# A uniform offset of 192 bytes for all split weights in SBUF

## The chip, the core and the metric

One core of one Trainium2 chip runs the whole program in one launch. The metric is the device time of that core in microseconds, from repeated runs of the same program; the profile is taken in one more execution of it.

## What is computed

The input is x of 256 tokens by 1024 features, float32. There are two layers. Each has a token mixer and a gated feed-forward net (FFN), each behind an RMS norm and added back to x; a last norm ends it.

```python
for i in range(2):
    h = rmsnorm(x, mix_norm[i])
    x = x + (short_conv_mixer(h) if i == 0 else moba_attention(h))
    x = x + conv_ffn(rmsnorm(x, ffn_norm[i]), w_up[i], w_conv[i], w_down[i])
return rmsnorm(x, final_norm)
# short_conv_mixer: b, c, v = split(h @ w_in); (b * causal_conv3(c * v)) @ w_out
# conv_ffn: g, u = split(causal_conv3(h @ w_up)); (silu(g) * u) @ w_down      (2816 wide)
# moba_attention: 16 heads of 64, rotary positions; with 256 tokens there is
#   one block, so it is plain causal softmax attention
```

## The kernel before

Activations lie with features on the 128 partitions and 256 tokens along the free dimension. Float32 accuracy is reached with three float32r products: weight and activation are each split into a high part (rounded to float32r) and a low part (the rest), and `passes` (line 304) issues high x high, high x low and low x high into the same PSUM bank.

The weights come as units of 128 x 1024 floats (the first eleven are smaller), two units to a load (`load_chunk`, line 154; four chunks are in flight). `split_next` (line 174) splits one unit: ScalarE writes `hi`, VectorE writes `lo`. The splits live in `SPLITS` = 5 buffers each. A matmul takes 128 columns of a unit, 512 bytes per partition, as its stationary operand (its weights) and streams 256 columns of an activation. Two products do it the other way round, with 512 columns of a weight unit moving past 128 columns of an activation: v of the attention (`v_stage`, line 645) and the down-projection of layer 1 (`TokenAccum`, line 351).

The stages follow each other in program order, and each engine works in that order (`InOrder`, line 87): the load phase with the first rounds of the mixer (`firsts`), then its rounds j = 2 to 7 (tiles cv and b, 48 and 24 products a round; mo is its output projection, 24 a round), the norm's sum of squares (`finish_norm`, tile ss: products with a 128 x 128 tile of ones, `ones_r`, as weights), the FFN of layer 0 (gu is the up-projection, 48 products for each of 22 j; fo is the down-projection, 24 for each j, which starts when j = 4 is through), the attention (q and k in tile qk, v, then scores s, transposes pt and value products o in plain float32, by four groups of heads; ao is its output projection), and the FFN of layer 1. The count of float32r products with 256 columns is 3992: 576 of cv and b, 192 of mo, 1056 of gu and 528 of fo in layer 0, 384 of qk, 192 of ao, 1056 of gu in layer 1, and 8 of ss. With 512 columns there are 360: 96 of v and 264 of fo in layer 1.

Where an operand begins in SBUF is set by `line` (line 135): it makes a tile that is `off` floats longer and rounds it up to `LINE` = 128 floats, and hands out the part behind `off`. The pools begin at a multiple of 512 bytes, so a tile's place relative to such a multiple is its `off`. For weights that is `WEIGHTS_AT` (line 37), by the kind of unit; for activations it is 0 everywhere. `ones_r` happens to begin 384 bytes behind a multiple. In bytes:

| products | stationary operand begins at | moving operand begins at |
|---|---|---|
| cv, b (and the load phase) | 64 | 0 |
| mo | 128 | 0 |
| gu, layer 0 | 192 | 0 |
| fo, layer 0 | 256 | 0 |
| q / k | 320 / 384 | 0 |
| v | 0 | 256 |
| ao | 448 | 0 |
| gu, layer 1 | 480 | 0 |
| fo, layer 1 | 0 | 128 |
| ss | 384 | 0 |

Since 128 columns are 512 bytes, every slice of a unit has the offset of the unit. All instructions carry line 97 in the profile (the helper `InOrder` issues them), so they are told apart by the names of their tiles.

Of the kernel before, what the change touches and what calls it, by code (L numbers as in the profile page):

```python
# [9 lines left out]
F32 = mybir.dt.float32  # L10
F32R = mybir.dt.float32r
# [3 lines left out]
P = 128  # L15
D = 1024
T = 256
# [7 lines left out]
U = 1024  # L25
# [2 lines left out]
NG = 4  # L28
GROUPS = 4
LOADS = 4  # L30
SPLITS = 5
NBIG = 14
NT = 10
LINE = 128


WEIGHTS_AT = {"first": 16, "in": 16, "out": 32, "up0": 48, "down0": 64, "q": 80, "k": 96, "v": 64, "o": 112, "up1": 120, "down1": 32}
INPUTS_AT = {0: 0, "out": 0, 1: 0, "down0": 0, 2: 0, "o": 0, 3: 0, "down1": 0}
NPS = 7
WARM = 8  # L40

# [32 lines left out]
PLAN = weight_plan()  # L74
# [39 lines left out]
def trunk(ctx: ExitStack, tc: tile.TileContext, x, wall, small, ropes, masks, final, out):  # L114
# [15 lines left out]
    rope = cp.tile([P, 3, T], F32, name="rope")  # L130
    mk = cp.tile([P, P + T], F32, name="mk")
    ones = cp.tile([P, P], F32, name="ones")
    ones_r = cp.tile([P, P], F32R, name="ones_r")

    def line(pool, w, off=0, dtype=F32, **kw):

        return pool.tile([P, -(-(off + w) // LINE) * LINE], dtype, **kw)[:, off : off + w]

    def gain(i, m):
        return gn_c[:, i * ND + m : i * ND + m + 1]  # L140
# [11 lines left out]
    raw, hi, lo = {}, {}, {}  # L152
# [21 lines left out]
    def split_next():  # L174
        u = state["split"]
        if u >= NU:
            return
        state["split"] += 1
        c, o = CHUNK_OF[u]
        while state["dma"] <= min(c + LOADS - 1, len(CHUNKS) - 1):  # L180
            load_chunk()
        w = WIDTH[u]
        src = raw[c][:, o : o + w]
        kind = PLAN[u][0] + (str(PLAN[u][1]) if PLAN[u][0] in ("up", "down") else "")
        hi[u], lo[u] = (
            line(wp, U + 127 - WEIGHTS_AT[kind], WEIGHTS_AT[kind], F32R, name=f"{n}{u}", tag=n, bufs=SPLITS)[:, :w]
            for n in ("hi", "lo")
        )
        if u < 2:
            V.tensor_copy(hi[u], src)  # L190
            if u == 0:
                scaled(0, (0,), nm0)
                split_next()
                for v, part in ((0, src), (1, raw[0][:, P : 3 * P])):
                    V.tensor_sub(lo[v], part, hi[v].bitcast(F32))
            return
        S.activation(hi[u], src, AF.Copy)
        V.tensor_sub(lo[u], src, hi[u].bitcast(F32))
# [10 lines left out]
    def spawn(*gens):  # L209
        tasks.extend(gens)  # L210
# [43 lines left out]
    def scaled(i, ms, nm):  # L254

        for m in ms:
            xh, xl = (
                line(ap_, T, INPUTS_AT[i], F32R, name=f"x{c}{i}_{m}", tag=f"x{c}{m}", bufs=1)
                for c in "hl"
            )  # L260
            S.activation(xh, xslice(m), AF.Copy, scale=gain(i, m))
            V.scalar_tensor_tensor(
                xl, xslice(m), gain(i, m), xh.bitcast(F32), op0=ALU.mult, op1=ALU.subtract
            )
            nm.xh[m], nm.xl[m] = xh, xl
# [12 lines left out]

    def table(func):

        t = line(ap_, 1, name="table", tag="table", bufs=1)
        S.activation(t, ones[:, 0:1], func)

    def finish_norm(i, nm, squared=False, cols=False, tag="b"):

        ps = bank(f"ss{i}", tag=tag)
        for part, total in enumerate(nm.total):
            kw = {"start": False, "stop": part == 1, "skip_group_check": True}
            E.matmul(ps[:, 0, :], ones_r, total, **{**kw, "start": part == 0})
            for t in range(2 if cols else 0):  # L290
                E.matmul(
                    ps[:, 1, 2 * t : 2 * t + 2], total[:, t * P : (t + 1) * P], ones_r[:, 0:2], **kw
                )
        n = T + 4 if cols else T
        rms = line(ap_, T + 4, name=f"rms{i}", tag="rms", bufs=1)
        ss = ps.rearrange("p a t -> p (a t)")[:, :n]
        S.activation(rms[:, :n], ss, AF.Sqrt, bias=eps, scale=1.0 / D)
        nm.r = line(ap_, T + 4, name=f"rstd{i}", tag="rstd", bufs=2)
        V.reciprocal(nm.r[:, :n], rms[:, :n])
        if squared:  # L300
            nm.r2 = ap_.tile([P, T], F32, name=f"rstd2{i}", tag="rstd2", bufs=1)
            V.tensor_mul(nm.r2, nm.r[:, :T], nm.r[:, :T])
# [131 lines left out]
    def pair_tile(name):  # L434
        return ap_.tile([P, 2, T], F32, name=name, tag="big", bufs=NBIG)

    def split_tiles(name, kind):
        return tuple(
            line(ap_, T, INPUTS_AT[kind], F32R, name=name + c, tag="ps" + c, bufs=NPS) for c in "hl"
        )  # L440

    def taps(y, src, w):
# [4 lines left out]


    V.memset(ones, 1.0)
    eps = cp.tile([P, 32], F32, name="eps")[:, 0:1]  # L450
    V.memset(eps, EPS)
    V.tensor_copy(ones_r, ones)
    o = NG * ND
# [31 lines left out]
    def mix_b(j, b_ps, in_y, wait=1):  # L485
        for _ in range(wait):
            yield
        yb = half_tile(f"yb{j}")
        V.tensor_mul(yb, b_ps[:, 0, :], in_y[0])
        yield  # L490
        ys[j] = split_tiles(f"ys{j}", "out")
        split_act(*ys[j], yb)

    firsts = [(bank(f"cv{j}", tag="a"), bank(f"b{j}", tag="a")) for j in range(2)]
# [55 lines left out]
    def ffn(layer, nm, i, then):  # L550
        acc, ps = (TokenAccum if then is None else Accum)(f"fo{layer}"), {}
        gus = {}

        def whole(j):
            gn, y = pair_tile(f"gn{layer}_{j}"), pair_tile(f"gy{layer}_{j}")
            s, p = half_tile(f"s{layer}_{j}"), half_tile(f"p{layer}_{j}")
            V.tensor_mul(gn, gus[j], nm.r[:, None, :T].to_broadcast([P, 2, T]))
            yield
            for h in range(2):
                taps(y[:, h, :], gn[:, h, :], lambda t: ffn_tap(layer, t, h, j))  # L560
            yield
            S.activation(s, y[:, 0, :], AF.Silu)
            V.tensor_mul(p, s, y[:, 1, :])
            yield
            ps[j] = split_tiles(f"ps{layer}_{j}", f"down{layer}")
            split_act(*ps[j], p)

        for j in range(NF):
            if layer == 0 and j == 2:
                Q.dma_start(rope, ropes)  # L570
                Q.dma_start(mk, masks)
            gu = gus[j] = bank(f"gu{layer}_{j}")
            wg, wu = unit(("up", layer, 0, j)), unit(("up", layer, 1, j))
            if j == 0:
                for ks in ((0, 1), (2, 3), (4, 5), (6, 7)):
                    project(gu[:, 0, :], wg, nm, ks)
                    project(gu[:, 1, :], wu, nm, ks, start=False)
                slot()
                slot()
            else:  # L580
                project(gu[:, 0, :], wg, nm)
                slot()
                project(gu[:, 1, :], wu, nm, start=False)
                if j == 1:
                    finish_norm(i, nm)
                    table(AF.Silu)
                    spawn(whole(0))
                spawn(whole(j))
                slot()
            if j >= LAG_FFN:  # L590
                acc.add(("down", layer, j - LAG_FFN), ps[j - LAG_FFN], j == LAG_FFN, False)
                slot()
        for j in range(NF - LAG_FFN, NF - 2):
            acc.add(("down", layer, j), ps[j], False, False)
            slot()
        while tasks:
            slot(0)
        table(AF.Sqrt)
        acc.finish(
            [("down", layer, j) for j in (NF - 2, NF - 1)],  # L600
            [ps[j] for j in (NF - 2, NF - 1)],
            then,
        )
# [89 lines left out]
    def softmax(g, ps):  # L693
        sm = [pair_tile(f"sm{g}_{h}").rearrange("p a t -> p (a t)") for h in range(4)]
        mx, nmx, sums, inv = (
            line(ap_, 8, name=f"{n}{g}", tag=n) for n in ("mx", "nmx", "sums", "inv")
        )
        parts = [(2 * h + t, h, slice(c0, c1)) for h in range(4) for c0, c1, t in SPANS]
        for c, h, cols in parts:
# [33 lines left out]
    def values(g, now=False):  # L733
        pt = pts.pop(g)
        o = bank(f"o{g}")
        for e in range(2):
            for t in range(2):
                for h in (2 * e, 2 * e + 1):
                    E.matmul(
                        o[h % 2 * HD : (h % 2 + 1) * HD, e, t * P : T],  # L740
                        vt[t][:, 4 * g + h, :],
                        pt[h][:, T * t : T * t + (T if t == 0 else P)],
                        start=e == 0 and t == 0,
                        stop=t == 1,
                        skip_group_check=True,
                    )
        hl = [
            line(ap_, 2 * T, INPUTS_AT["o"], F32R, name=f"o{c}{g}", tag=f"o{c}{g}", bufs=1)
            .rearrange("p (a t) -> p a t", a=2)
            for c in "hl"  # L750
        ]
        for e in range(2):
            os_[2 * g + e] = tuple(v[:, e, :] for v in hl)

        def split_values():
            split_act(*hl, o)
            yield

        spawn(split_values())
        if now:  # L760
            next(tasks[-1])
# [145 lines left out]
```

## Time and profile before

| | us |
|---|---|
| median of 3 runs | 583.34 (582.89 to 583.95) |
| the profiled execution | 582.72 |
| its span, first to last instruction | 580.9 |
| mean granted clock of TensorE | 0.998 of full speed |

Three views matter here. The page's head gives each engine's busy time. The waits of an engine say what held it up. The chain that ended last, in order of time, merges like instructions that follow each other on it, and says of each run when it starts, how long it takes and how many there are: a run's length divided by its count is the time from one matmul's start to the next. (The duration that the profile gives for one matmul, some 278 ns, overlaps with its neighbours.)

### The profile page before, as it was taken

What the parts mean: (1) busy time and instruction counts of PE and PEld (TensorE: products, weight loads), DVE (VectorE), ACT (ScalarE), POOL (GpSimd) and SP (SyncE); (2) the same over time, 40 slices, a digit from 0 to 9 for tenths busy, and PEclk for the clock granted to TensorE, in tenths of its full rate; (3) what the DMA queues carried; (4) which work ended last, traced back from release to release, by engine and by line L of the source; (5) the groups of instructions that cost most, each with busy time, mean ns of one, the idle gap of its engine ahead of it and who ended that gap; (6) DMA issues with size and microseconds to landing.
All of it is one profiled execution on the core that took longest, in us unless ns stands there. A gap on an engine that the chain in (4) does not pass through costs nothing.

```text
span 580.9 us, 11291 instructions
## 1 busy us (share of the span) xinstructions
PE 573.9 (99%) x4628; PEld 552.9 (95%) x4628; DVE 470.4 (81%) x783; ACT 338.0 (58%) x556; POOL 8.7 (2%) x12
## 2 busy tenths in 40 slices
PE   9999999999999999999999999999999999999996
PEld 8999999999999999999989997999999999999984
DVE  6997768899978877886998887577998878877883
ACT  7654447567655555555846656565665555555543
POOL 0022010000000000000000000000000000000000
PEclk9999999999999999999999999999999999999999
DMA  8957561746645546455264344463566455564301
GB/s 305 371 206 247 189 217 73 259 155 243 247 162 212 185 178 217 155 210 192 103 230 156 119 146 146 146 228 116 186 225 220 161 209 177 186 210 159 140 1 72
DMA packets 17188, 106.86 MB, mean 184 GB/s; under 512 B 1904, under 2 KB 3056, under 8 KB 4976
## 3 DMA queue, kind: packets, MB, share of 16 engines
q1 hardware_dynamic: 16704, 105.60, 51.1%
q8 instruction: 36, 0.59, 0.4%
q10 hardware_dynamic: 432, 0.54, 0.3%
q14 instruction: 16, 0.13, 0.1%
HBM read 105.09 MB, written 1.05 MB: 183 GB/s over the span
## 4 chain that ended last, share of the span: by engine, by line
PE 97%; DMA 1%; SPq 0%; ACT 0%; DVE 0%; issue 0%; ACTq 0%
PE gu L97 42%; PE fo L97 22%; PE qk L97 8%; PE cv L97 7%; PE ao L97 4%; PE mo L97 4%; PE v L97 4%; PE b L97 4%; PE pt L97 1%; PE s L97 1%; PE o L97 1%; DMA raw<-wall 1%; SPq L97 0%; PE ss L97 0%; ACT hi L97 0%; ACT of L97 0%
## 5 line engine op out<-in xcount | busy, mean ns | idle before, releaser
L97 ACT ACTIVATE hi<-raw 128x1024 fp32r<-128x1024 f32 (+2 forms) x199 | 205.5, 1041 | 155.3 <-PE gu L97 83.6
L97 DVE TENSOR_TENSOR lo<-raw,hi 128x1024 fp32r<-128x1024 f32 (+3 forms) x201 | 239.9, 1200 | 61.1 <-ACT hi L97 60.8
L97 PE MATMUL gu<-xl,hi 128*128 128x256 f32 x704 | 195.8, 278 | 0.0
L97 PE MATMUL gu<-xh,hi 128*128 128x256 f32 x704 | 195.7, 278 | 0.0
L97 PE MATMUL gu<-xh,lo 128*128 128x256 f32 x704 | 195.7, 278 | 0.0
L97 PEld LDWEIGHTS gu<-xh,hi 128*128 128x128 f32 x704 | 132.3, 188 | 0.7
L97 PEld LDWEIGHTS gu<-xl,hi 128*128 128x128 f32 x704 | 132.2, 188 | 0.7
L97 PEld LDWEIGHTS gu<-xh,lo 128*128 128x128 f32 x704 | 132.2, 188 | 0.0
L97 DVE SCALAR_TENSOR_TENSOR gy<-gn,sm,gy 128x255 f32<-128x255 f32 (+1 forms) x176 | 80.8, 481 | 3.1
L97 ACT ACTIVATE gy<-gn,sm 128x256 f32<-128x256 f32 x88 | 39.3, 497 | 6.4 <-DVE gn L97 6.4
L97 PE MATMUL qk<-xh,hi 128*128 128x256 f32 x128 | 36.4, 284 | 0.0
L97 PE MATMUL qk<-xl,hi 128*128 128x256 f32 x128 | 35.8, 280 | 0.0
L97 PE MATMUL qk<-xh,lo 128*128 128x256 f32 x128 | 35.8, 280 | 0.0
L97 DVE TENSOR_TENSOR gn<-gu,rstd 128x512 f32<-128x512 f32 x44 | 30.1, 689 | 6.5 <-PE gu L97 6.5
L97 PE MATMUL cv<-xh,hi 128*128 128x256 f32 x128 | 33.3, 281 | 0.4 <-ACT hi L97 0.4
L97 PE MATMUL cv<-xl,hi 128*128 128x256 f32 x128 | 32.9, 278 | 0.0
L97 PE MATMUL cv<-xh,lo 128*128 128x256 f32 x128 | 32.8, 277 | 0.0
L97 PEld LDWEIGHTS qk<-xh,hi 128*128 128x128 f32 x128 | 24.2, 189 | 0.5 <-issue 0.3
L97 PEld LDWEIGHTS qk<-xl,hi 128*128 128x128 f32 x128 | 24.1, 188 | 0.0
L97 PEld LDWEIGHTS qk<-xh,lo 128*128 128x128 f32 x128 | 24.1, 188 | 0.0
L97 PEld LDWEIGHTS cv<-xh,hi 128*128 128x128 f32 x128 | 23.1, 189 | 0.7 <-ACT hi L97 0.6
L97 ACT ACTIVATE s<-gy 128x256 f32<-128x256 f32 x44 | 17.9, 406 | 9.4 <-DVE gy L97 9.2
(474 smaller groups left out, 1081.7 us busy)
## 6 DMA issues: line engine op xcount, KB each, us to landing
raw<-wall SPq DMA_DIRECT2D x95, 1024.0 KB, 4.7
raw<-wall SPq DMA_DIRECT2D x6, 384.0 KB, 6.7
xt<-x SPq DMA_DIRECT2D x3, 256.0 KB, 6.1
out<-of SPq DMA_DIRECT2D x3, 256.0 KB, 2.1
raw<-wall SPq DMA_DIRECT2D x3, 192.0 KB, 4.2
gain_row<-final SPq DMA_DIRECT2D x1, 512.0 KB, 5.7
rope<-ropes SPq DMA_DIRECT2D x1, 384.0 KB, 5.9
out<-of ACTq DMA_DIRECT2D x1, 256.0 KB, 2.4
```

The costliest lines, as they stand in the source:

```text
L97: r = f(*args, **kw)
```

## The change

All split weights get one offset. The table `WEIGHTS_AT`, the table `INPUTS_AT` and the helper `line` go. Instead the tiles of constants that come first are sized so that what follows falls into place: `eps` is made 80 floats (320 bytes) long and is allocated ahead of `ones_r`, so that `ones_r`, and with it everything behind it in the pools of constants and weights, begins 192 bytes beyond a multiple of 512; the tile `table`, the first of the activations' pool, is 80 floats long too, and 192 + 320 = 512 brings all activations back to a multiple. The raw (unsplit) weights, `vt` and `gain_row` also lie at 192 now. Without the padding a split buffer is 4096 bytes instead of 4608, and there are six of each kind instead of five. The order of instructions on each engine and their number are as before; the inner function `whole` of the FFN is renamed `gated`, since `whole` now names the helper that rounds a tile up to 128 floats.

```diff
-SPLITS = 5
+SPLITS = 6
-LINE = 128
-WEIGHTS_AT = {"first": 16, "in": 16, "out": 32, "up0": 48, "down0": 64, "q": 80, "k": 96, "v": 64, "o": 112, "up1": 120, "down1": 32}
-INPUTS_AT = {0: 0, "out": 0, 1: 0, "down0": 0, 2: 0, "o": 0, 3: 0, "down1": 0}
...
     ones = cp.tile([P, P], F32, name="ones")
+    eps = cp.tile([P, 80], F32, name="eps")[:, 0:1]
     ones_r = cp.tile([P, P], F32R, name="ones_r")
-    def line(pool, w, off=0, dtype=F32, **kw):
-        return pool.tile([P, -(-(off + w) // LINE) * LINE], dtype, **kw)[:, off : off + w]
+    def whole(pool, w, **kw):
+        return pool.tile([P, -(-w // 128) * 128], F32, **kw)[:, :w]
...
-        kind = PLAN[u][0] + (str(PLAN[u][1]) if PLAN[u][0] in ("up", "down") else "")
-        hi[u], lo[u] = (
-            line(wp, U + 127 - WEIGHTS_AT[kind], WEIGHTS_AT[kind], F32R, name=f"{n}{u}", tag=n, bufs=SPLITS)[:, :w]
-            for n in ("hi", "lo")
-        )
+        hi[u] = wp.tile([P, w], F32R, name=f"hi{u}", tag="hi", bufs=SPLITS)
+        lo[u] = wp.tile([P, w], F32R, name=f"lo{u}", tag="lo", bufs=SPLITS)
...
-        t = line(ap_, 1, name="table", tag="table", bufs=1)
+        t = ap_.tile([P, 80], F32, name="table", tag="table", bufs=1)[:, 0:1]
...
-    eps = cp.tile([P, 32], F32, name="eps")[:, 0:1]
```

## Rows read from the trace of the kernel before

**Rows 1.** The page's head: busy us, share of the span, count.

```profile
span 580.9 us, 11291 instructions
...
PE 573.9 (99%) x4628; PEld 552.9 (95%) x4628; DVE 470.4 (81%) x783; ACT 338.0 (58%) x556; POOL 8.7 (2%) x12
```

**Rows 2.** The waits of TensorE: us in total, times, longest us.

```profile
PE busy L97 <- DVE eps L97: 1.1, 1, 1.1
PE cv L97 <- ACT hi L97: 0.4, 1, 0.4
```

**Rows 3.** The chain in order of time: start us, length us, what, count.

```profile
3.53 5.06 DMA raw<-wall
...
22.36 5.65 PE cv L97 x48
...
53.18 5.46 PE cv L97 x48
...
83.40 11.39 PE mo L97 x96
94.78 11.31 PE gu L97 x96
...
126.16 5.44 PE gu L97 x48
...
264.72 14.40 PE fo L97 x120
279.12 8.51 PE qk L97 x72
291.17 10.90 PE v L97 x48
...
367.31 21.40 PE ao L97 x180
388.71 11.31 PE gu L97 x96
...
421.75 5.60 PE gu L97 x48
...
561.43 13.94 PE fo L97 x60
```

**Rows 4.** The timeline of TensorE from 10 to 22: start us, us, instruction.

```profile
10.29 0.28 PE L97 MATMUL b<-xh,hi 128*128 128x256 f32 x1
...
21.85 0.28 PE L97 MATMUL b<-xh,lo 128*128 128x256 f32 x1
21.97 0.28 PE L97 MATMUL ss<-totalh,ones_r 128*128 128x256 f32 x1
22.08 0.28 PE L97 MATMUL ss<-totall,ones_r 128*128 128x256 f32 x1
```

**Rows 5.** The timeline of TensorE behind waits in qk and ao.

```profile
322.20 0.28 PE L97 MATMUL qk<-xl,hi 128*128 128x256 f32 x1
...
324.81 0.28 PE L97 MATMUL qk<-xh,hi 128*128 128x256 f32 x1
...
364.45 0.28 PE L97 MATMUL ao<-ol,hi 128*128 128x256 f32 x1
...
365.58 0.28 PE L97 MATMUL ao<-oh,lo 128*128 128x256 f32 x1
```

**Rows 6.** Groups of splits: the page's; then by tile, min/median/max ns, two stretches each.

```profile
L97 ACT ACTIVATE hi<-raw 128x1024 fp32r<-128x1024 f32 (+2 forms) x199 | 205.5, 1041 | 155.3 <-PE gu L97 83.6
...
L97 DVE TENSOR_TENSOR lo<-raw,hi x52: 1214/1224/1227, 127.9 to 263.0; 128x1024 fp32r<-128x1024 f32 x52
L97 DVE TENSOR_TENSOR lo<-raw,hi x52: 1211/1224/1227, 421.8 to 559.6; 128x1024 fp32r<-128x1024 f32 x52
L97 ACT ACTIVATE hi<-raw x52: 1042/1061/1063, 125.5 to 261.9; 128x1024 fp32r<-128x1024 f32 x52
L97 ACT ACTIVATE hi<-raw x51: 1044/1060/1063, 421.4 to 558.5; 128x1024 fp32r<-128x1024 f32 x51
```

More of the change, by code (lines that the diff above doesn't have):

```diff
@@ L256, in scaled @@
         for m in ms:
[L257 to L260, printed above, removed]
+            xh = ap_.tile([P, T], F32R, name=f"xh{i}_{m}", tag=f"xh{m}", bufs=1)
+            xl = ap_.tile([P, T], F32R, name=f"xl{i}_{m}", tag=f"xl{m}", bufs=1)
             S.activation(xh, xslice(m), AF.Copy, scale=gain(i, m))
@@ L294, in finish_norm @@
         n = T + 4 if cols else T
-        rms = line(ap_, T + 4, name=f"rms{i}", tag="rms", bufs=1)
+        rms = whole(ap_, T + 4, name=f"rms{i}", tag="rms", bufs=1)
         ss = ps.rearrange("p a t -> p (a t)")[:, :n]
         S.activation(rms[:, :n], ss, AF.Sqrt, bias=eps, scale=1.0 / D)
-        nm.r = line(ap_, T + 4, name=f"rstd{i}", tag="rstd", bufs=2)
+        nm.r = whole(ap_, T + 4, name=f"rstd{i}", tag="rstd", bufs=2)
         V.reciprocal(nm.r[:, :n], rms[:, :n])
@@ L435, in pair_tile, with split_tiles @@
         return ap_.tile([P, 2, T], F32, name=name, tag="big", bufs=NBIG)
-    def split_tiles(name, kind):
+    def split_tiles(name):
         return tuple(
-            line(ap_, T, INPUTS_AT[kind], F32R, name=name + c, tag="ps" + c, bufs=NPS) for c in "hl"
+            ap_.tile([P, T], F32R, name=name + c, tag="ps" + c, bufs=NPS) for c in "hl"
         )
@@ L490, in mix_b @@
         yield
-        ys[j] = split_tiles(f"ys{j}", "out")
+        ys[j] = split_tiles(f"ys{j}")
         split_act(*ys[j], yb)
@@ L552, in ffn, with gated @@
         gus = {}
-        def whole(j):
+        def gated(j):
             gn, y = pair_tile(f"gn{layer}_{j}"), pair_tile(f"gy{layer}_{j}")
@@ L564, in whole @@
             yield
-            ps[j] = split_tiles(f"ps{layer}_{j}", f"down{layer}")
+            ps[j] = split_tiles(f"ps{layer}_{j}")
             split_act(*ps[j], p)
@@ L586, in ffn @@
                     table(AF.Silu)
-                    spawn(whole(0))
-                spawn(whole(j))
+                    spawn(gated(0))
+                spawn(gated(j))
                 slot()
@@ L695, in softmax @@
         mx, nmx, sums, inv = (
-            line(ap_, 8, name=f"{n}{g}", tag=n) for n in ("mx", "nmx", "sums", "inv")
+            whole(ap_, 8, name=f"{n}{g}", tag=n) for n in ("mx", "nmx", "sums", "inv")
         )
@@ L746, in values @@
                     )
[L747 to L751, printed above, removed]
+        hl = [ap_.tile([P, 2, T], F32R, name=f"o{c}{g}", tag=f"o{c}{g}", bufs=1) for c in "hl"]
         for e in range(2):
```

## The prediction

> **What bounds the kernel now.** I read the page from the top. TensorE is busy for 573.9 of the span of 580.9 us, VectorE for 470.4 [rows 1]. Next the waits of TensorE: in the whole span it waits 1.1 us for a constant and 0.4 us for the first splits [rows 2]. So no load, no split and no evacuation sets the time; the spacing of the 4628 matmuls on TensorE does. The third view is the chain that ended last, in order of time. It gives runs of like matmuls as a start, a length and a count, and length by count is the pitch, the time from one matmul's start to the next. All float32r products of 256 columns have one shape (128x128 weights, 128x256 moving), yet their pitch differs [rows 3]: 5.46/48 = 113.7 ns and 5.44/48 = 113.3 in the fastest runs, 117.7 and 117.8 in others, 118.6 in mo, 120.0 in fo of layer 0. There are 3992 such products and 360 with 512 columns (226.7 at best: the 10.90 us for 48 of v are 227.1 and hold the way in; 232.3 in fo of layer 1). 1 ns on each of the 3992 is 4 us of the end. 113.3, 120.0 and 226.7 are 17, 18 and 34 times 6.67 ns, so I take 113.3 for the floor of a 256-column product here and 226.7 for one of 512.
>
> **What the pitch hangs on.** Put the byte offsets of the weights before (table in the text ahead) beside [rows 3]. Moving activations are at a multiple of 512 throughout; what differs is the offset of the 128 weight columns that are loaded while the matmul before still streams. Weights at 256 (fo, layer 0): 120.0 in every run. At 128 (mo): 118.6. At 320 and 384 (the run of qk): 118.2. At 192 (gu, layer 0): 113.3 in 17 blocks of 48, but 117.8 in the first 240 products. At 64 (cv, b): 117.7 in the block at 22.36, 113.7 in the one at 53.18. At 448 (ao): 118.9 over 180. At 480 (gu, layer 1): 117.8 at first, 116.7 later. Two things follow. An odd multiple of 64 (64, 192, 320, 448) is the only kind of offset at which 113.3 is seen; at 128, 256 and 384 no run stays there. And at an odd multiple there are two lasting paces, 113.3 and 117.8, and which one holds depends on what went before, since the same tiles at the same addresses run at both. The changes of pace show that. The products at 64 run at 113.3 from 10.29 to 21.85 (102 of them in 11.56 us); then come the two products of the norm's sum, whose ones lie at 384 [rows 4], and behind them cv at 64 runs at 117.7 and stays so for two rounds of j [rows 3]. Coming from fo (256) gu at 192 is at 113.3, coming from mo (128) it is at 117.8 [rows 3]. After a wait, ao at 448 once runs 364.45 to 365.58 for ten products, 113.0, and three microseconds later, from 367.31 on, 118.3 for good; qk at 320 settles at 322.20 to 324.81 for 23 products, 113.5 [rows 5].
>
> **The skill's rule against it.** The Trainium skill, "TensorE: Matmul & The Clock Gate", section "Step-by-step: what each phase is for", says that TensorE has two independent read ports into SBUF and that loading the next tile's weights takes nothing from the running matmul. By that the offset of weights is worth 0 and the time would stay at 583.3. The trace disagrees: 120.0 against 113.3 in alternate blocks of one loop, with moving tiles at the same offset.
>
> **The change, part by part.** It puts every split weight at 192, the ones of the sums at 192 too, and leaves activations at multiples of 512. So every 256-column product stands as gu of layer 0 does now, and nothing along the way changes the relation, the sums of the norms included. Count times distance to the floor, stage by stage [rows 3, 4]:
> - cv and b of j = 2 and 3: 144 x (117.7 - 113.3) = 0.6 us
> - mo: 192 x (118.6 - 113.3) = 1.0
> - gu of layer 0, first 240: 240 x 4.5 = 1.1; the other 816 are at the floor: 0
> - fo of layer 0: 528 x 6.7 = 3.5
> - qk: 384, of which some 72 (three blocks behind a wait, as the one from 322.20) are at the floor: 312 x 4.9 = 1.5
> - ao: (21.40 - 0.11 for the wait it holds)/180 = 118.3, 180 x 5.0 = 0.9
> - gu of layer 1: 240 x 4.5 + 816 x (116.7 - 113.3) = 1.1 + 2.7
> - fo of layer 1, now moving weights of 512 columns: 264 x (232.3 - 226.7) = 1.5
> - v: 96 x 0.4, less than 0.1
>
> The sum is 14.0 us. Nothing of it is hidden, because TensorE waits for nobody [rows 2]; against the profiled execution's 582.72 us (span 580.9) it gives 568.7, against the median of 583.34 some 569.3. That is the floor, and ways into it cost something: after each wait three to five products are slower, the scores, transposes and value products of the attention break the pace in each of its four groups, and a block of 24 that comes out of such a break at 117.8 loses 0.1 us. For these I keep back 1.7 us, by choice: some two thirds of what qk and ao are to gain (2.4 us). That is 571.0.
>
> The unknown inside this is 512 columns moving at 192 with weights at 0: no row has it. The bounds are 226.7 (v, moving at 256, once it has settled) and twice 117.8 = 235.6; the row of fo, moving at 128, lies between at 232.3 [rows 3]. So 264 products are worth from -1.5 to +0.9 us; I take the floor, since at odd multiples of 64 the narrow products have it too. Leaving out a gain on the products now at the floor, no row goes below it.
>
> The small parts. Six buffers of splits in place of five: ScalarE's idle time before a split is mostly for gu to release a buffer (155.3 us idle in all, 83.6 of it so) [rows 6], and nobody on the path waits for splits [rows 2], so a sixth buffer is worth 0; without that cover it would be the 0.4 us of the first wait. The splits' own offsets: hi and lo take 1061 and 1224 ns in layer 0 (weights at 192, 256) and 1060 and 1224 in layer 1 (480, 128) [rows 6], so 192 costs VectorE and ScalarE nothing. VectorE's 470.4 us become 83% of a span of 568.6. The raw weights move to an offset of 192 with the rest. The loads set only the start, 5.06 us of the chain [rows 3]; 5% on that either way is 0.3 us.
>
> **Rivals.** (1) The slow pace in the last FFN: gu of layer 1 comes out of fo's 512-column products in a new way each block. If all 1056 hold 117.8 and fo goes to 235.6, that costs 4.7 + 2.3 us over the forecast: 576 to 578. For: at 480 that stage does not settle at the floor [rows 3]. Against: from fo of layer 0 gu went into the floor 17 times of 17. (2) The slow pace from the start. The pace of everything to the end of layer 0 (2352 products) is settled at the last wait of the load phase, near 9.6 us, since nothing after it would disturb it. If 117.8 holds there, 2352 x 4.5 = 10.5 us are lost: 571.0 + 10.5 = 581.5. (3) The other side of zero: (1) and (2) together, the products caught at 117.8 everywhere. Then the 1320 or so that are at 113.3 today (432 of cv and b, 816 of gu, 72 of qk) lose 4.5 ns each, 5.9 us; gu of layer 1 loses 0.9 and its fo 0.9, fo of layer 0 still gains 1.2 and mo 0.2: 583.3 + 6.3, about 589.5. It decides at one point, the pitch of the third or fourth product after the last wait of the load phase: 113.3 or 117.8. Of four returns after a full wait at odd multiples of 64, three went to the floor (64 behind the wait at 9.6, 320 at 322, 448 at 364) and one to the slow pace (448 at 367) [rows 3 to 5]; coming out of products at another offset it was slow more often (after the sum, after mo). (4) The offset is not the cause, and the blocks differ by something that goes with the stage (the skill's rule, or PSUM banks): 583.3. Against it: the changes inside cv and inside gu without a change of stage.
>
> **How the numbers follow.** Forecast 571.0 (569 to 574): 0.46. Rival 1 (575 to 578): 0.20. Rival 2 (579.5 to 582.5): 0.13. Rival 3 (586 to 590): 0.12. Rival 4 (583): 0.09. Under 0.2% of the time, 1.2 us, a measurement cannot tell a difference. So faster: 0.46 + 0.20 + 0.12 = 0.78; same: 0.09 + 0.01 = 0.10; slower 0.12. The range takes in the forecast, rival 1 and rival 2: from the floor less the 0.3 us of the start, 569.0, to 582.5.
>
> **What would show it.** In the chain of the changed kernel every run of cv, b, mo, gu, fo of layer 0 should have one pitch, 5.44 us for 48, and the two products of ss should stand in it without changing it. fo of layer 0 at 120 would say that the offset is not the cause. 5.65 for 48 from about 10 us on means rival 2. For layer 1, blocks of gu at 5.44 and 13.6 us for the last 60 of fo, against 5.65 and 14.1 (rival 1). The hi and lo groups should keep 1.06 and 1.22 us, and the waits of TensorE should stay under 2 us in all; a new wait there for ScalarE or a load would make the prediction wrong in a way that none of these cases covers.

## The result and the profile after

The changed kernel takes 587.51 us (median of 4 runs, 587.45 to 587.62) against 583.21 for the kernel before on the same chip (582.89 to 583.95): a ratio of 1.0079, interval 1.0065 to 1.0093. It is slower by 4.3 us, where 571.0 was forecast and 582.5 was the upper end of the range. Some of the kernels further down fall, from one run to the next, into two groups of times some 10 us apart; the granted clock of TensorE is 0.997 to 1.000 of full speed in both, a ratio is then that of the lower group, and why there are two is part of what has to be explained.

The head of the page after, in the columns of [rows 1], and the waits of TensorE, as [rows 2]:

```profile
span 585.7 us, 11250 instructions
PE 579.1 (99%) x4628; PEld 558.4 (95%) x4628; DVE 463.9 (79%) x783; ACT 338.0 (58%) x556; POOL 11.3 (2%) x12
```

```profile
PE busy L92 <- DVE eps L92: 1.1, 1, 1.1
```

TensorE has the same 4628 matmuls, in this view one wait, for the same constant as before, and its busy time is 5.2 us longer; the granted clock is 0.998 in both profiled executions. So the loss is pitch. The chain in order of time after (start us, length us, what, count), for [rows 3]:

```profile
22.98 5.65 PE cv L92 x48
...
85.17 11.31 PE mo L92 x96
96.47 11.31 PE gu L92 x96
...
127.80 5.65 PE gu L92 x48
...
269.14 14.13 PE fo L92 x120
283.27 8.48 PE qk L92 x72
...
295.26 11.20 PE v L92 x48
...
370.80 21.40 PE ao L92 x180
392.20 11.31 PE gu L92 x96
...
425.25 5.65 PE gu L92 x48
...
566.15 14.02 PE fo L92 x60
```

The reader divides: 5.65/48 and 11.31/96 are 117.7 and 117.8 ns, 14.13/120 is 117.8, and so in every block to the end of layer 0. Up to there nothing is at 113.3 any more, and nothing at 118.6 or 120.0 either: one offset, one pitch, but the slow one of the two. (In the attention one stretch is fast: behind the break at 326.60, 72 products of qk settle at 113.3.) The starts set beside [rows 3] give the account of the 4.8 us by which the span grew:

| stretch | before to after, us |
|---|---|
| load phase (up to the cv of j = 2) | +0.62 |
| rounds of the mixer (cv, b, mo) | +1.07 |
| first FFN up to its last fo run | +2.73 |
| last fo run of layer 0 | -0.27 |
| attention (qk to the start of gu) | -0.66 |
| gu of layer 1 and the part of fo between | +1.23 |
| last fo run of layer 1 | +0.08 |

(22.98 - 22.36; then (96.47 - 94.78) - 0.62; (269.14 - 264.72) - (96.47 - 94.78); and so on.) Two stretches became shorter: the last fo run of layer 0, whose products go from 120.0 to 117.8, and the attention. The attention's gain goes with the sixth buffer. ScalarE's idle time before the splits into hi falls from 155.3 us [rows 6] to 14.1:

```profile
L92 ACT ACTIVATE hi<-raw 128x1024 fp32r<-128x1024 f32 (+2 forms) x199 | 203.3, 1036 | 14.1 <-DMA raw<-wall 5.1 <-PE cv L92 5.0 <-PE v L92 2.4
```

Before, a split on ScalarE had to wait 2.20 us until products of qk released a buffer, and the exponentials of the softmax (sm) stand behind that split in ScalarE's order. VectorE waits 1.94 us for them and ends the scaling of sm at 329.74 + 1.93 = 331.67, while the transposes of sm into pt have begun at 330.51 and must wait for the last of it; after, they follow each other freely. Before (start us, length us, instruction, in brackets the engine's idle time ahead and what ended it), then after:

```profile
324.90 1.06 ACT L97 ACTIVATE hi<-raw 128x1024 fp32r<-128x1024 f32 x1 [2.20 <-PE qk L97]
...
329.50 0.20 DVE L97 RECIPROCAL inv<-sums 128x8 f32<-128x8 f32 x1 [1.94 <-ACT sm L97]
329.74 1.93 DVE L97 TENSOR_SCALAR sm<-sm,inv 128x256 f32<-128x256 f32 x8
...
330.51 1.77 PE L97 MATMUL pt<-mk,sm 128*128 128x128 f32 x12
```

```profile
334.80 1.47 PE L92 MATMUL pt<-mk,sm 128*128 128x128 f32 x12
```

By the chain the four runs of 12 transposes take 1.31, 1.60, 1.64 and 1.80 us before and 1.31 each after: 1.1 us gained. All six traces with six buffers have 5.24 us for the four, all fourteen with five have 6.26 to 6.70. (Six: the changed kernel, e1 to e4, e16.) The place of the raw weights, `vt` and `gain_row` differs between the two groups as well, and no run separates that from the buffers. Without this gain the loss would be some 5.4 us.

### The profile page after: what moved, and what is told of

Its sections match the earlier page's. It is cut to its first block, busy times and chain, and to the rows that moved or that the text cites. A ratio compares the mean times of both kernels' runs of the same rounds, so it can differ in the third digit from the quotient of the medians.

```text
span 585.7 us, 11250 instructions
## 1 busy us (share of the span) xinstructions
PE 579.1 (99%) x4628; PEld 558.4 (95%) x4628; DVE 463.9 (79%) x783; ACT 338.0 (58%) x556; POOL 11.3 (2%) x12
## 4 chain that ended last, share of the span: by engine, by line
PE 99%; ACT 0%; DVE 0%; issue 0%
PE gu L92 42%; PE fo L92 21%; PE cv L92 8%; PE qk L92 8%; PE ao L92 4%; PE b L92 4%; PE mo L92 4%; PE v L92 4%; PE s L92 1%; PE o L92 1%; PE pt L92 1%; PE busy L92 1%; PE ss L92 0%; ACT of L92 0%; DVE of L92 0%; ACT sq L92 0%
## 5 line engine op out<-in xcount | busy, mean ns | idle before, releaser
L92 ACT ACTIVATE hi<-raw 128x1024 fp32r<-128x1024 f32 (+2 forms) x199 | 203.3, 1036 | 14.1 <-DMA raw<-wall 5.1
```

The source lines that it names most:

```text
L92: r = f(*args, **kw)
```

## The experiments

Eighteen experiments; e9 and e10 run the kernel of e6 again, e16 that of e2. "After" in a diff's heading means that the edit is made on the changed kernel, "before" on the kernel before; offsets in the code are floats (16, 32, 48, 64 floats are 64, 128, 192, 256 bytes), in the text bytes. The history theory of the expectations: at odd multiples of 64 two paces last, and which one holds depends on what went before. The offset theory: 192 throughout, or what else the change moved, gives 117.8 by itself. Fast and slow stand for 113.3 and 117.8 ns; a passage is a stretch of products at another offset. Pitches of a few products are read from the start times in the trace, which has them to 1 ns.

**e1: the changed kernel, with the eleven units of the load phase at 64.**

```diff
+        off = 96 if PLAN[u][0] == "first" else 0
-        hi[u] = wp.tile([P, w], F32R, name=f"hi{u}", tag="hi", bufs=SPLITS)
+        hi[u] = wp.tile([P, off + w], F32R, name=f"hi{u}", tag="hi", bufs=SPLITS)[:, off : off + w]
```

> The changed kernel, but the eleven units of the load phase (first) begin at 64 instead of 192; all other weights and the ones stay at 192. History theory: the load phase settles at 113.3 ns as in the kernel before, and since nothing changes the relation afterwards, some 2150 products from 22 to 285 us at 192 run at 113.3 instead of 117.8: 10 us less than the changed kernel, about 577, with blocks of 48 gu at 5.44 us in layer 0 and 5.65 still in layer 1. Offset theory (a uniform 192, or the six buffers and raw weights at 192, gives 117.8 by itself): only the load phase gains, 587.0.

Measured: 577.14 us (577.14, 577.13, 576.82 and one of 586.61), ratio 0.9902 [0.9886, 0.9919]. Its chain:

```profile
22.74 5.44 PE cv L92 x48
...
93.46 10.88 PE gu L92 x96
...
123.61 5.44 PE gu L92 x48
...
259.61 13.60 PE fo L92 x120
```

The instructions are those of the changed kernel, and from j = 2 on the tiles lie where they lie there. What differs is over by 22.5 us, and 2.2 thousand products behind it run at 113.3 instead of 117.8. That is the history theory's answer.

**e2, e4: 64 and 448 throughout** (after; `eps` 48 or 144 floats, `table` 112 or 16).

> The changed kernel with 64 in place of 192 throughout (weights, ones, raw, vt, gain_row; activations still at multiples of 512). History theory: the load phase settles at 113.3 as at 64 in the kernel before, the sums no longer break it, so everything up to the attention runs at 113.3: 577, and 570 to 572 if layer 1 finds the fast pace too. Offset theory: uniform weights at an odd multiple of 64 are what gives 117.8: 587.5.

> The changed kernel with 448 in place of 192 throughout. 448 and 192 are 256 apart, and in the kernel before ao at 448 and gu at 192 had the same pattern at the slow pace. If the paces repeat every 256 bytes, history theory: the same two paces, and since loads and splits come at the same times most likely the same slow one, 587.5; a fast entry would show 577. Offset theory without such a period: any time between 570 and 596, with one pitch from start to end.

At 64 two runs at 573.92 and 574.28, two at 583.55 and 584.96; ratio of the lower group 0.9852 [0.9832, 0.9872]. In the profiled run, one of the lower group, all of layer 0 is at 113.3, with ao and the first 240 products of gu in layer 1; the rest of that stage is at 117.9:

```profile
359.87 20.61 PE ao L92 x180
...
412.43 5.66 PE gu L92 x48
...
552.80 13.77 PE fo L92 x60
```

At 448 the time is 587.60 (587.53 to 587.82), ratio 1.0085 [1.0068, 1.0101], and its blocks are those of the changed kernel: 448 and 192, 256 bytes apart, behaved alike.

**e3: ones of the norms' sums at 256** (after; `eps` 96 floats and a pad of 112 behind the ones).

> The changed kernel with the ones of the norms' sums at 256 instead of 192; all weights at 192. Only the 8 products of ss stand otherwise. In the kernel before, gu at 192 was fast each time it came out of products at 256. History theory: the two products of ss near 22.9 us turn the slow pace into the fast one, so cv from there on is at 113.3 (5.44 for 48) until the next ss at 107: between 577 and 585 by how many of the three sums leave the fast pace behind (layer 0 alone is worth 10 us). Offset theory: 587.5, all blocks at 5.65.

587.59 us (587.29 to 587.79), ratio 1.0083 [1.0068, 1.0098], every block at 5.65 for 48. Two products at 256 did not turn the slow pace. The hope was that they would; so not every passage by another offset turns it.

**e5: the kernel before, with all weights and the ones at 192** and nothing else of the change (five buffers, raw weights at multiples of 512).

> The kernel before with every weight at 192 and the ones at 192: the offsets of the changed kernel, without its six buffers (five of 4608 bytes) and without raw weights, vt and gain_row at 192 (they stay at multiples of 512). History theory: offsets and entry as in the changed kernel, so 587.5, or 577 in runs where the load phase ends in the fast pace. If buffers or the place of the raw weights matter, something else: up to the 583 of the kernel before.

Runs from 578.1 to 588.79, median 588.72 (4 runs; no ratio, before 582.49). The profiled run (span 576.3) has all of layer 0 at 113.3. So one program comes out at either pace, a surprise, and both groups of times come without the sixth buffer and with the raw weights in their old place: neither is needed for the loss. The offset theory falls with it. (The upper group of this kernel has no trace; e9 below, which differs by 24 products, shows its pace. The upper runs are 1.2 us above the changed kernel: the transposes again, 6.48 us here against 5.24.)

**e6, e9, e10: e5 with the 24 products of one unit of j = 2 at 256** (`at = 64 if PLAN[u] == ("in", 0, 1, 2) else WEIGHTS_AT[kind]`).

> As e5, but one unit of 199, the first after the load phase (cv of j = 2, 24 products), lies at 256. Products at 256 ran at 120.0 in the kernel before, and gu at 192 behind them was fast 17 times of 17. History theory: those 24 products run at 120 (0.16 us lost), and all behind them to the end of layer 0 run at 113.3 whatever the load phase left: 577 in every run, 10 us less than e5. Offset theory: as e5 plus 0.1.

> The kernel of the run before last in this group once more (all weights and ones at 192, the unit of the first round behind the load phase at 256), for one profile as it falls: its times lie near 578 or near 588.8, and only an execution near 578 has been seen in a trace. If an execution near 588.8 is caught: by the theory that one block at another offset sets the pace anew and always to the same side, 113.3 ns must hold for some time behind the 24 products at 256 and be lost later, at a place that the chain shows. By the theory that a block at another offset leaves the pace as it came (slow in, slow out; fast in, fast out), the blocks ahead of the 24 products are at 117.8 already, and all behind them too: 5.65 us for each 48 to the end of layer 0.

> The same kernel, a second execution in a profile: the same two answers, or the other pace beside the first for a comparison of the load phase of the two.

e6: ten runs, four from 576.87 to 579.18 and six from 586.89 to 589.56; ratio of the lower group 0.9924 [0.9906, 0.9942]. The 24 products did not bring all runs to the lower group, a miss. e9 (588.72 us) and e10 (578.80 us) are one execution each of this kernel, and caught both answers. e9's chain, then e10's:

```profile
22.89 5.71 PE cv L97 x48
...
31.43 5.65 PE cv L97 x48
```

```profile
23.00 5.59 PE cv L97 x48
...
31.32 5.44 PE cv L97 x48
```

In both the load phase ends at 117.8. In e10 the products at 256 run at 120, 120, 120 and leave at 113, 113, 114; in e9 they run in a cycle of 121, 120, 124, 117, 118, also 120 on average, and leave at 118, 117, 118. So there are two paces at 256 too, with one mean, and the pace behind went with the one that was taken. My two alternatives were each half wrong: the passage neither always turns the pace nor always leaves it.

**e7: the kernel before, only the ones at 192.**

> The kernel before with one part of the change alone: the ones of the norms' sums at 192 instead of 384, all weights as before. History theory: the sum after the load phase no longer breaks the fast pace, so cv and b of j = 2 and 3 (144 products) run at 113.3 instead of 117.8: 0.6 us less than before, 582.2 to 582.5; the later sums stand in stretches that are slow already and change nothing. Offset theory: no change, cv stays at 5.65 for 48.

581.91 us (581.33 to 582.88, 10 runs) against 582.49, ratio 0.9986 [0.9975, 0.9996], at the edge of what times can tell; the chain tells it plainly. The two rounds of cv behind the sum, at 5.65 in [rows 3], are at 113.3:

```profile
22.33 5.44 PE cv L97 x48
...
30.49 5.44 PE cv L97 x48
```

That is the prediction's first term alone, 0.6 us.

**e8: e6 with v and the last down-projection moving at 256 and the last unit of ao at 256.**

> As e6, and for layer 1: the last unit of ao at 256 too, and the units that move 512 columns (v, down-projection of layer 1) at 256 instead of 192. v at 256 settled at 226.7 in the kernel before. History theory: gu of layer 1 starts at 113.3 (240 products, 1.1 us), fo of layer 1 runs at 226.7 instead of 233.7 (1.8 us); whether the 816 products of gu behind it are fast is open (3.6 us): 574 if not, 570.5 if so. Offset theory: 587, less 1.8 for fo.

Runs from 575.51 to 586.0, median 585.33. Span of the profiled run 573.7:

```profile
382.88 10.88 PE gu L97 x96
...
414.80 5.65 PE gu L97 x48
...
554.53 13.62 PE fo L97 x60
```

The first gu of layer 1 at 113.3 behind 24 products at 256, and 512 columns at 227.0 (13.62/60) when they move at 256; gu between them stays at 117.7.

**e11: e5 with the down-projection of layer 0 at 256.**

> All weights and the ones at 192, only the down-projection of layer 0 at 256, so that 24 products at 256 stand ahead of every pair of gu's products from j = 4 on, as they do in the kernel before. By the theory that 256 sets the pace anew, gu of layer 0 at 113.3 in all its 17 blocks in every run; only cv, b, mo and the first 240 of gu can differ between runs (1008 products x 4.5 = 4.5 us): groups near 580.5 and 585. By the theory that 256 leaves the pace as it came: groups near 580.5 and some 10 us above it less nothing for fo, near 589. By the offsets alone: one group.

One group, 584.76 to 586.46, ratio 1.0052 [1.0037, 1.0067]:

```profile
108.42 16.96 PE gu L97 x144
125.38 2.87 PE fo L97 x24
128.25 5.44 PE gu L97 x48
```

Slow up to the first fo, fast in all 17 blocks behind it. The account closes: 588.73 (the upper runs of e5) - 816 x 4.45 ns + 528 x 2.2 ns (fo at 120 instead of 117.8) = 586.3.

**e12 to e15: mixtures** (before, with this table; e12 and e13 have `up0` and `up1` at 48, `down0`, `v` and `down1` at 64, q, k, o at 48, the ones at 192 bytes and the last unit of ao at 64).

```diff
-WEIGHTS_AT = {"first": 16, "in": 16, "out": 32, "up0": 48, "down0": 64, ...}
+e12: {"first": 16, "in": 16, "out": 64, "up0": 48, "down0": 64, ...}
+e13: {"first": 16, "in": 16, "out": 16, "up0": 48, "down0": 64, ...}
+e14: {"first": 16, "in": 16, "out": 16, "up0": 48, "down0": 48, ...}; ("down", 0, 0 to 3) and ("o", 7) at 64
+e15: as e14, "up1": 16; ("o", 7) at 32
```

> A mixture that keeps what was the same in every run of the kernel before and takes gains that were seen singly: load phase and cv, b, mo at 64, ones at 192, gu of both layers and q, k at 192, the down-projection of layer 0 at 256, v and the down-projection of layer 1 moving at 256, the last unit of ao at 256. From rows: cv and b 0.6, mo 1.0, the first 240 of gu 1.1, qk 0.6, the first 240 of gu in layer 1 1.1, fo of layer 1 1.4, less 0.9 for gu of layer 1 at 117.8 in place of 116.7: 4.9 us, some 578.3. If the pace of the load phase at 64 falls either way in this kernel too, a second group 4.5 us above it, near 583 (the blocks at 256 in the FFN set it anew) or 8 us above it (they don't).

> The mixture before it, with mo at 64 like cv and b (there mo lay at 256, though the text on it said 64). By the theory that 64 by way of 256 to 64 loses the pace: cv and b of j = 4 to 7 back at 113.3 (288 products x 4.4 = 1.3 us) and mo at 113.3 for 120 (192 x 6.7 = 1.3 us): 580.5 - 2.6 = 577.9. By the theory that the slow rounds there were chance: the same for mo alone, 579.2. If the load phase at 64 can come out slow in this kernel too: a second group 1008 x 4.4 = 4.4 us above.

> The same with the down-projection of layer 0 at 256 for its first four j alone, at 192 behind them. If the pace that the four passages set lasts until the attention, as it lasts through the whole of layer 0 where all weights are at 192: 432 products x 6.7 = 2.9 us less than the one before, some 575.0, and since the four passages come behind the load phase, a slow load phase costs no more than 4.4 us. If the pace is lost when fo goes to 192: gu of layer 0 at 117.8, 2.9 less 3.7 and 1.9 less gain for fo, some 577.7 to 578.7.

> The same as e14 with gu of layer 1 at 64 instead of 192 and the last unit of ao at 128 instead of 256 (24 products at 128 ahead of 64 kept 113.3 in the kernel before). If coming back from 512 moving columns at 256 to weights at 64 finds the fast pace: 816 x 4.5 = 3.7 us less than e14, some 571.3. If it stays at 117.8 there: as e14; and if the passage by way of 128 fails too, 1.1 us more than e14.

e12: 580.51 us (580.04 to 581.1), ratio 0.9959 [0.9945, 0.9973]. Its mo lay at 256, not at 64 as its text says, and that taught something:

```profile
30.48 5.44 PE cv L97 x48
...
38.64 2.88 PE mo L97 x24
41.51 5.65 PE cv L97 x48
...
95.59 10.88 PE gu L97 x96
```

From 64 by way of 24 products at 256 back to 64 the fast pace was lost; from the 96 at 256 into gu at 192 it was found. With mo at 64 instead of 256 cv of e13 was expected to keep it. Five runs of e13 lie from 577.6 to 578.88, as expected (577.9); ratio over all six 0.9932 [0.991, 0.9953]. The profiled run is the one left, 581.81, and shows on the timeline of TensorE and VectorE what made it longer:

```profile
38.33 0.41 DVE L97 TENSOR_TENSOR ys0l<-yb,ys0h 128x256 fp32r<-128x256 f32 x1
...
38.73 0.28 PE L97 MATMUL mo<-ys0h,hi 128*128 128x256 f32 x1
38.80 0.19 PEld L97 LDWEIGHTS mo<-ys0l,hi 128*128 128x128 f32 x1
38.85 0.34 PE L97 MATMUL mo<-ys0l,hi 128*128 128x256 f32 x1
39.02 0.28 PE L97 MATMUL mo<-ys0h,lo 128*128 128x256 f32 x1
```

VectorE ends ys0l at 38.74, and the second product of mo needs it. Its weight load starts at 38.80, some 60 ns later than the fast pace has it. TensorE loses these 60 ns, and then 4.45 ns on every product: b ahead of it is at 113, 113, 114, mo behind it at 118, 117, 118, and that stays so through four rounds of the mixer, the first 240 of gu, the first passage by fo and the 48 of gu behind it; the second passage by fo (at 256) turns it back. That is 768 products, 3.4 us; without them the run would be at 578.4, and the median of the other five is 578.5. In e14, whose load phase is 0.3 us longer, ys0l was ready and nothing broke.

e14: 575.2 us (575.03 to 576.41), ratio 0.9876 [0.9858, 0.9894], 575.0 expected. The pace was fast already ahead of the four passages by way of 256, so the trace does not show that four are enough to mend a slow one; it does show that the pace lasts through the 432 products of fo at 192 behind them:

```profile
93.59 10.88 PE gu L97 x96
...
121.02 2.88 PE fo L97 x24
123.90 5.44 PE gu L97 x48
...
252.22 2.72 PE fo L97 x24
254.94 5.44 PE gu L97 x48
```

This version beats the kernel before by 1.2% (582.97 us on its chip) and the changed kernel by 2.0% (0.9876/1.0079), and still has five buffers; the sixth's 1.1 us were not tried on it. e15: 576.17 us (576.06 to 577.05), ratio 0.9889 [0.9874, 0.9904]: gu of layer 1 at 64 is at 5.66 for 48, no better than at 192. Its load phase came out of the wait at 10.2 us slow, at 64, and the two products of the sum (192) turned it fast.

**e16: e2 once more.**

> The kernel with 64 throughout once more, for one profile as it falls (its times lay near 574 or near 584.5; only one near 574 has been seen in a trace). If one near 584.5 is caught: by the theory that the return from the waits of the load phase falls to either side, the blocks of cv from the load phase on are at 117.8 and stay there to the end of layer 0. By the theory that a return at 64 always finds 113.3: the blocks of the load phase are at 113.3 and the pace is lost later, at a place that the chain shows.

574.15 us and a load phase at 113.3: the lower group again, so the question about the upper one stays without an answer. But this run has the hold-up of e13 at the same product, and a longer one. VectorE ends ys0l at 39.02, and TensorE waits for it:

```profile
38.57 0.28 PE L92 MATMUL mo<-ys0h,hi 128*128 128x256 f32 x1
...
39.07 0.39 PE L92 MATMUL mo<-ys0l,hi 128*128 128x256 f32 x1 [0.23 <-DVE ys0l L92]
```

The second product of mo starts 505 ns behind the first, in place of 113. The next ones follow after 222, 120, 116, 116, 114, 114 ns, and then the pace is 113.3 again, to the end of layer 0. So a hold-up at 64 can also leave the fast pace behind: it is a new draw, and not always the slow side.

**e17, e18: the kernel before with weights and ones at 64 throughout, without and with mo's first two units at 128.**

```diff
-        at = 32 if PLAN[u] == ("o", 7) else WEIGHTS_AT[kind]
+        at = 32 if PLAN[u] in [("o", 7), ("out", 0, 0), ("out", 0, 1)] else WEIGHTS_AT[kind]
```

> From the kernel before, everything at 64 (weights, ones, the moving weights of v and of the last FFN), the last unit of ao at 128. In e13 the pace went from 113.3 to 117.8 where the weights of mo's second product were 64 ns late, and stayed there. By the theory that any short hold-up can turn the pace and that it then lasts, this kernel has two groups of times, near 573.5 and, where mo's first products knock it, up to 2208 x 4.45 = 9.8 us above. By the theory that at 64 the fast pace always comes back, one group near 573.5.

> The same with the first two units of mo at 128, through which cv and b at 64 came to 113.3 in the kernel before whatever their pace was ahead of them. If that passage sets the pace anew, one group near 573.5 + 48 x 5.3 ns = 573.8 in every run; only the load phase and j = 2 and 3 can differ (some 250 products x 4.45 = 1.1 us). If a slow pace goes through it: a second group near 583, as in the kernel without it.

(The moving weights of v and of the last FFN lie at 256 in both, not at 64.) e17: 574.76, 574.82, 575.12 and 585.34, two groups as expected; ratio of the lower 0.986 [0.9844, 0.9877]. e18: 575.16, 576.18, 576.23, 576.23, one group, ratio 0.9877 [0.986, 0.9893]. Its chain shows the passage at work:

```profile
22.96 5.65 PE cv L97 x48
...
39.92 2.85 PE mo L97 x24
42.77 5.46 PE cv L97 x48
...
94.61 10.88 PE gu L97 x96
```

The load phase ends slow, at 64; behind 24 products at 128 the pace is fast, and stays so. The 1.4 us to e17's lower group are the load phase and two rounds of cv and b at 117.8, and the 48 products at 128. Four runs in one group do not set this kernel apart from e17, which had three of four in its lower group; what speaks for the passage is that trace.

## Why the prediction was wrong

**Right.** That TensorE's pitch is the time: e1 and the changed kernel differ by 10.4 us, with no wait between them. The Trainium skill, "TensorE: Matmul & The Clock Gate", section "Step-by-step: what each phase is for", says that loading the next tile's weights takes no read bandwidth from the running matmul. By that, e1 and the changed kernel, which differ only in where eleven units lie, would take the same time; the runs are 577.14 and 587.51. That two paces last and history chooses was right as well, and so was "nothing along the way changes the relation": from 6.8 us to the end of layer 0 nothing in the changed kernel did. The term for the sum of the norms was 0.6 us, and e7 measured it alone. The floor of 569 was not reached by any run; the best groups are at 574 (e2) and 575 (e17), and gu of layer 1 is most of what is missing (816 x 4.5 = 3.7 us): at 64, 192 and 448 it never ran at 113.3 between two blocks of 512 columns.

**The step that failed** is the choice of the pace in the load phase. The prediction counted returns from a full wait at odd multiples of 64, found three of four at the floor, and gave the pace at 192 to the same side, though none of the four was at 192 and its own rows had 192 slow behind mo. The trace of before holds eight such returns, of which five were fast: it left out two fast ones of qk (303.5 and 338.0) and two slow ones (316.0 and 332.0). What came was rival 3, given 0.12. It named the deciding point, the pitch of the third or fourth product after the wait, and there the changed kernel shows 118, 117, 118. Counted over all traces, the last wait of the load phase was left at 113.3 in 9 of 11 at 64 (before, e1, e2, e7, e12, e13, e14, e16, e17; slow in e15, e18), and in 1 of 9 at 192 or 448 (e5; slow in the changed kernel, e3, e4, e6, e8 to e11). A return at 192 was a different draw from one at 64, and the whole of layer 0 hung on it. The breaks in the attention lean the same way: in the kernels with qk and ao at one offset, the pace settled at 113.3 behind 15 of 28 breaks at 64 and behind 23 of 98 at 192 or 448, though many of these repeat one pattern from trace to trace.

**A second step:** 512 columns moving at 192 with weights at 0. The bounds were 226.7 and 235.6, I took the lower end; the last row of the chain gives 233.7 (14.02/60), and v 233.3. Against the sum that is 264 x 7.0 = 1.8 us. Measured in the last run of fo, by the offset of the moving operand: 227.0 at 256 (e8), 229.5 at 64 (e2), 232.3 at 128 (before), 233.7 at 192. The row to go by was the nearer one, 128.

**A third step:** the sixth buffer at 0. The prediction argued from the waits of TensorE, which show two, both in the load phase [rows 2]. The transposes' waits, 0.3 to 0.5 us each, are not in that view; they show only in the chain, as runs of pt that differ in length. They were worth 1.1 us: no split was waited for, but a split that waited for a buffer held up the softmax behind it on ScalarE, and through it VectorE, and both came onto the path for three short moments.

**The price of rival 3** was 6.3 us, against 4.8 by the spans. cv, b and gu of layer 0 cost what it said: 0.6 and 1.2 us, and 816 x 4.45 = 3.6. The rest is the attention, set at a loss of 0.3 and in truth a gain of 0.66 (1.1 for the transposes, less 0.5 for v at 192), and fo of layer 1, set at 0.9 where 264 x (233.7 - 232.3) is 0.4.

**What stays open.** What within TensorE makes the two paces; what of a wait decides between them, so that one program comes out at either, and why 64 leans one way and 192 the other; and whether the changed kernel ever comes out fast: in its runs, and in those of e3 and e4, it did not. For the upper groups of e1, e2 and e17, no run of which was caught in a trace, two causes are seen elsewhere: a hold-up at mo as in e13, and a load phase at 64 that comes out slow as in e15 and e18. An estimate from 4.45 ns on 2064 products from mo on, or on all 2352 from the load phase on, is 9.2 or 10.5 us. The runs lie 9.5 (e1), 9.4 and 10.9 (e2) and 10.5 us (e17) above their lower groups, so either may have been at work. And why the hold-up of e13 left the slow pace and the longer one of e16 the fast one is open too.

## What to carry to other kernels

Where TensorE is the bound, divide the runs of the chain by their counts before anything else; a few per cent of pitch can hang on the offset of the weights, and a mean over a stage hides that it is one of two paces. A pace that lasts must be made robust, not only reached: a loop that passes regularly by products at another offset, as the kernel before does, gets further chances to find the fast pace (e13 found it at the second passage), while a uniform layout mostly keeps what the last wait or hold-up gave it. Judge a layout by several runs, and look at the run that is longer.

## What the runs showed of the hardware

- A float32r product of 128x128 by 128x256 came every 113.3 or every 117.8 ns with the same tiles at the same addresses, for hundreds of microseconds at a stretch.
- Behind one weight load some 60 ns late the pace had changed from the fast to the slow (e13); behind one 0.5 us late at the same product it was fast again after some six products (e16).
- How the pace went through products at another offset, moving operands at multiples of 512:

| from, by way of, to | pace |
|---|---|
| 64, 2 at 384, 64 | fast to slow (before) |
| 64, 2 at 192, 64 | slow to fast (e15), fast to fast (e7, e12 to e14) |
| 64, 24 at 128, 64 | slow to fast, later fast to fast (before, e18) |
| 64, 24 at 256, 64 | fast to slow, later slow to slow (e12) |
| 192, 2 at 256, 192 | slow to slow (e3) |
| 192, 24 at 256, 192 | slow to fast (the first of before, e7 and e11, the second of e13, and e6, e8, e10); slow to slow (e9, and the first of e13); fast to fast (the later ones of before, e7, e11 and e13, and all in layer 0 of e12, e14 and e15) |
| 64 to 192 | fast to fast (e1, e14), slow to slow (e13) |

- The mean pitch does not tell the state: at 256 two cycles, 120 throughout and 121, 120, 124, 117, 118, have the same mean and leave different paces behind.
